# Whole float32 products in place of split ones in decode and retention, and the softmax's chunk factors made by ScalarE alone

## The chip, the cores and the metric

The kernel runs on one core of one Trainium2 chip. The metric is the device time of one execution in microseconds (us); smaller is better. The kernel before took 3410.53 us (median of 3 runs, 3404.25 to 3414.77). Engines are called PE (TensorE, with PEld for its weight loads), DVE (VectorE), ACT (ScalarE), POOL (GpSimd) and SP (SyncE, which issues every DMA here).

## The reference

One layer of a streaming encoder, for a prompt of 2048 tokens and for a batch of 8 decode sequences of 16 new tokens each. All is float32.

```python
h = rms_norm(x, g_norm);  z = h @ w_in
fq, fk, fv, ff, fg, rq, rk, rv, rg, mq, mg, gl = split(z)
# A) forgetting attention: 8 heads x 64, decode has 2048 cached keys
s = fq @ fk.T * 64**-0.5 + c_q - c_k            # c = cumsum(log sigmoid(ff + b_f)), causal
fox_o = softmax(s) @ fv
# B) retention: 4 heads, key width 128, value width 256, in chunks
inter = (q @ s) * dec_q
scores = (q @ k.T) * dmask;  intra = scores @ v
s_new = exp(log_g * L) * s + (k * dec_k).T @ v
# M) attention into 256 memory tokens, 4 heads x 128
mem_o = softmax(mq @ mk.T * 128**-0.5) @ mv
merged = sum_i gate_i * ((branch_i * silu(gate path)) @ w_p_i)
y = x + merged @ w_out
```

The outputs are y, the new keys and values, the log forget gates and the new retention states, for prompt and decode.

## The kernel before

The program has three parts in time. The first makes the input projection for all 17 token tiles (16 of the prompt, one with the 128 decode tokens). The last merges the branches and multiplies by the output weights for the last four of five blocks of tokens. Neither is touched by the change. Between them lies the middle part, where two lanes are woven together: the left lane runs `forget`, `mem_prompt`, `decode_mem`, `decode_fox` and then the first output block; the right lane runs `retention` (16 prompt chunks, then the decode chunk in `sample`) and then `fox`, the prompt's forgetting attention. `weave` advances the lane that is behind by its given total; the builder then orders the instructions of every engine by its own estimate of their times, so that instructions of the lanes lie between one another in each engine's queue, and each engine takes its queue strictly in order. All DMAs go through SP's queue.

TensorE takes float32 data in two ways here. A tile of type F32R is multiplied in one instruction, at reduced precision. To keep precision, an operand is split: h is the value rounded to F32R (a cast by ACT, or by POOL for the decode's values), l = value - h (a subtraction on DVE or POOL), and `mm3` (lines 226 to 228) or `mm3r` (lines 232 to 234) add three products, h by h, h by l and l by h. `split` (line 202 the cast, line 205 the subtraction) is a helper, so these lines stand for many tiles, and the tile's name tells them apart. A tile of type F32 is multiplied as a whole; in the program that is one matmul, and in the profile it is two MATMUL records. Before the change only a few products are whole: the retention's scores (line 1062) and some small sums (lines 1428, 1433, 1451, 1564, 1699).

What the change touches:

- `ret_parts`, lines 1035 to 1056: the transposed q and k of a chunk (`qt`, `kt`), and the split q, k and v (`qh`, `ql` lines 1046 and 1047, `knh`, `knl` lines 1050 and 1051, `vh`, `vl` lines 1054 and 1055). `ret_scores`: the scores in PSUM (`rm`), masked into `sm`, split into `smh`, `sml` (lines 1067 and 1068). `retention.unit`: outputs in PSUM `ry` (line 1138, six products per head), state update in `rm` (three products per head) and `st` (line 1152), which is split again into `sth`, `stl` for the next chunk. `sample` does the same for the 8 decode states, two heads at a time.
- `softmax_scale`, lines 1248 to 1263: where a row's keys come in several chunks of 512, each chunk has its own maximum; DVE takes the difference to the row's maximum (line 1258), ACT the exponential (line 1259), DVE goes on.
- `decode_fox`, lines 1405 onward: for each sequence b, four chunks of 512 cached keys: 16 transposes (line 1500) in groups of four, a split of each group (`dkh`, `dkl`), three products each into `ys`, a softmax, transposes of the probabilities (line 1531) and their split `dpr`, and the product with the values, split by POOL (`dvh` line 1542, `dvl` line 1543), in four matmuls of 256 columns per 128 keys (line 1548).
- `decode_mem`: the same with 256 memory tokens (`mkh`, `mkl`, `mvh`, `mvl`, `mpr`).

## Time and profile before

| | |
|---|---|
| median of 3 runs | 3410.53 us (3404.25 to 3414.77) |
| the profiled execution, its own time | 3406.5 us |
| its span, first to last instruction | 3404.7 us |
| granted TensorE clock, mean of full speed | 0.974 |
| first part (projection), us from the span's start | 0 to 1686 |
| middle part, retention and memory attention | 1686 to 2052 |
| middle part, prompt and decode forgetting attention, first output block | 2052 to 2860 |
| last part (output blocks) | 2860 to 3404.7 |

The borders of the middle part are read from the first and last start of the tiles named above: the first retention transpose starts at 1683.5, the last of `decode_mem` at 2044.2, the last fox product at 2846.5, the second output block's products at 2883.7. The profile gives the busy time of an engine as the union of its instructions' times; matmuls overlap one another, and how much work PE has is rather told by the distance between the starts of matmuls that follow one another without a wait. A wait is put down to the instruction that ended it. The rows themselves stand further down.

### The profile page before, as it was taken

What the parts mean: (1) busy time and instruction counts of PE and PEld (TensorE: products, weight loads), DVE (VectorE), ACT (ScalarE), POOL (GpSimd) and SP (SyncE); (2) the same over time, 40 slices, a digit from 0 to 9 for tenths busy, and PEclk for the clock granted to TensorE, in tenths of its full rate; (3) what the DMA queues carried; (4) which work ended last, traced back from release to release, by engine and by line L of the source; (5) the groups of instructions that cost most, each with busy time, mean ns of one, the idle gap of its engine ahead of it and who ended that gap; (6) DMA issues with size and microseconds to landing.
All of it is one profiled execution on the core that took longest, in us unless ns stands there. A gap on an engine that the chain in (4) does not pass through costs nothing. (4 is left out here: it accounts for less than half of the span.)

```text
span 3404.7 us, 60285 instructions
## 1 busy us (share of the span) xinstructions
PE 3195.5 (94%) x22299; PEld 2997.7 (88%) x22299; DVE 2271.3 (67%) x3732; ACT 1743.5 (51%) x3404; POOL 1217.7 (36%) x1122
## 2 busy tenths in 40 slices
PE   6999999999999999999878888999999988999999
PEld 5998999999999999999868766888887888888899
DVE  7677676665565666565588877887777886545444
ACT  4453444555344555445468755767776764223222
POOL 4436443110220010220176443777776764100000
PEclk8999999999999999999999987999999999999999
DMA  4776566567557667667567765455654457676665
GB/s 166 230 246 201 180 209 198 190 211 253 168 167 215 203 212 244 205 192 220 192 198 230 243 195 162 153 157 162 179 179 148 129 151 224 184 223 204 191 188 166
DMA packets 628219, 660.94 MB, mean 194 GB/s; under 512 B 46060, under 2 KB 549252, under 8 KB 627860
## 3 DMA queue, kind: packets, MB, share of 16 engines
q1 hardware_dynamic: 627924, 657.08, 62.5%
q8 instruction: 176, 2.88, 0.3%
q14 instruction: 119, 0.97, 0.1%
HBM read 477.52 MB, written 179.41 MB: 193 GB/s over the span
## 5 line engine op out<-in xcount | busy, mean ns | idle before, releaser
L400 DVE TENSOR_TENSOR wl<-wr,wh 128x1024 fp32r<-128x1024 f32 (+1 forms) x386 | 568.4, 1476 | 286.9 <-ACT wh L399 282.1
L399 ACT CAST wh<-wr 128x1024 fp32r<-128x1024 f32 (+1 forms) x386 | 404.6, 1050 | 309.9 <-PE b L451 128.0
L449 PE MATMUL a<-wh,ho 128*128 128x256 f32 (+1 forms) x1432 | 408.4, 286 | 18.1 <-ACT gz L707 11.3
L450 PE MATMUL a<-wl,ho 128*128 128x256 f32 (+1 forms) x1432 | 406.3, 284 | 5.8 <-DVE wl L400 5.8
L451 PE MATMUL a<-wh,ho 128*128 128x256 f32 (+1 forms) x1432 | 407.0, 284 | 1.0 <-DVE ho L276 1.0
L428 POOL TENSOR_TENSOR wr<-wr 128x1024 f32<-128x1024 f32 (+1 forms) x72 | 202.1, 2806 | 270.0 <-DMA wr<-in_w_in 235.0
L451 PE MATMUL b<-wh,ho 128*128 128x256 f32 (+1 forms) x1032 | 290.5, 282 | 5.4 <-DVE ho L276 5.4
L449 PE MATMUL b<-wh,ho 128*128 128x256 f32 (+1 forms) x1032 | 291.3, 283 | 4.0 <-ACT wh L399 2.3
L221 ACT CAST wh<-wraw 128x1024 fp32r<-128x1024 f32 x120 | 123.3, 1049 | 334.9 <-DMA wraw<-in_w_p 131.4
L449 PEld LDWEIGHTS a<-wh,ho 128*128 128x128 f32 x1432 | 273.4, 191 | 22.1 <-ACT gz L707 13.7
L450 PE MATMUL b<-wl,ho 128*128 128x256 f32 (+1 forms) x1032 | 290.4, 282 | 0.5 <-DVE wl L400 0.5
L450 PEld LDWEIGHTS a<-wl,ho 128*128 128x128 f32 x1432 | 273.7, 191 | 6.3 <-DVE wl L400 6.3
L451 PEld LDWEIGHTS a<-wh,ho 128*128 128x128 f32 x1432 | 273.7, 191 | 1.5 <-DVE ho L276 1.5
L449 PE MATMUL a<-ho,wh 128*128 128x384 f32 (+1 forms) x768 | 252.6, 329 | 1.6 <-ACT gz L707 1.6
L450 PE MATMUL a<-ho,wh 128*128 128x384 f32 (+1 forms) x768 | 252.9, 329 | 0.0
L451 PE MATMUL a<-ho,wl 128*128 128x384 f32 (+1 forms) x768 | 252.1, 329 | 0.0
L460 ACT COPY kp<-a 128x256 f32<-128x256 f32 (+3 forms) x384 | 153.3, 404 | 183.5 <-PE a L451 182.0
L1334 ACT ACTIVATE pt<-sc,f_mx 128x512 f32<-128x512 f32 (+2 forms) x320 | 201.5, 631 | 73.2 <-DVE f_mx L1333 48.4
L1338 POOL TENSOR_SCALAR pt<-pt,f_f,f_nm 128x512 f32<-128x512 f32 (+3 forms) x288 | 208.6, 740 | 82.2 <-DVE f_nm L1262 28.9
L1333 DVE TENSOR_REDUCE f_mx<-sc 128x1 f32<-128x512 f32 (+2 forms) x320 | 192.6, 604 | 39.4 <-PE sc L1327 21.7
L205 DVE TENSOR_TENSOR pl<-tp,ph 128x512 fp32r<-128x512 f32 (+2 forms) x352 | 193.5, 562 | 34.6 <-ACT ph L202 33.0
L1745 POOL TENSOR_TENSOR gm<-gm,gm 128x512 f32<-128x512 f32 (+2 forms) x40 | 45.6, 1139 | 447.4 <-DVE gm L1743 447.3
(437 smaller groups left out, 9901.0 us busy)
## 6 DMA issues: line engine op xcount, KB each, us to landing
wr<-in_w_in SPq DMA_DIRECT2D x170, 512.0 KB
wraw<-in_w_p SPq DMA_DIRECT2D x80, 512.0 KB
dkt<-in_cache_fox_k SPq DMA_DIRECT2D x64, 512.0 KB
dvt<-in_cache_fox_v SPq DMA_DIRECT2D x64, 512.0 KB
wr<-sum_gl SPq DMA_DIRECT2D x48, 512.0 KB
wraw<-in_w_out SPq DMA_DIRECT2D x40, 512.0 KB
gtd<-gz SPq DMA_DIRECT2D x96, 192.0 KB
gt<-gtd SPq DMA_DIRECT2D x24, 768.0 KB
```

Source lines behind the costliest of these rows:

```text
L205: V.tensor_tensor(l, src, f32(h), ALU.subtract)
L221: S.copy(whv[:, i * hc:(i + 1) * hc], rv)
L399: S.copy(h, t)
L400: eng.tensor_tensor(l, t, f32(h), ALU.subtract)
L428: G.tensor_tensor(out, x, y, op)
L449: T.matmul(out, lh(c), rh(c), start=first and c == 0, stop=False, skip_group_check=True)
L450: T.matmul(out, lh(c), rl(c), start=False, stop=False, skip_group_check=True)
L451: T.matmul(out, ll(c), rh(c), start=False, stop=last and c == 3, skip_group_check=True)
L460: S.copy(t[nm], t["a"])
L1333: V.tensor_reduce(nmx[:, j, ci:ci + 1], sc[:, :w], AX.X, ALU.max, negate=True)
L1334: S.activation(pt[:, :w], sc[:, :w], AF.Exp, bias=nmx[:, j, ci:ci + 1], accum_out=l[:, j, ci:ci + 1])
L1338: G.tensor_scalar(pt, pt, fb, 0.5 if r is None else r[:, j:j + 1], ALU.mult, ALU.mult)
```

## The change

- Decode and retention multiply float32 tiles as whole products. The splits of q, k, v, scores, states, cached keys, cached values and probabilities go there, with the three or six products each; one whole product stands in their place (two MATMUL records each).
- The cached keys of both decode attentions are laid out transposed in the input arrays, on the host, so that the transposes of decode keys go. The DMA of a key tile has the same bytes, in contiguous runs of 2 KB (512 keys) instead of 4 KB, and 1 KB instead of 2 KB for the memory keys.
- The decode queries and new keys that arrive split (`dq`, `dk`, `qms`) are summed once on DVE.
- In `sample`, the masked keys (`kz`) and the placed queries (`qz`) are made by POOL, and the state update takes its decay factor on DVE as it adds.
- In `retention.unit` the state update is now issued ahead of the outputs, and there is one more step (`yield`) before a chunk is stored.
- `softmax_scale`: ACT makes the factor directly, exp(-nmx + nm), with the row's maximum as bias, one instruction per query block; DVE's difference goes.
- Some tiles have more buffers (`rk`, `rv` 4, `dkt` 4, `dvt` 4).

The core of the diff:

```diff
@@ -1032,41 +1032,25 @@
         dma(g, rgd[t * P:(t + 1) * P])
         return g
 
-    def ret_parts(rw, q, k, v):
+    def ret_turn(rw, q, k):
+
+        qt = rw.tile([P, 512], F32, name="qt", bufs=3)
...
-        S.copy(qh, qt)
-        G.tensor_tensor(ql, qt, f32(qh), ALU.subtract)
...
-        S.copy(vh, v)
-        G.tensor_tensor(vl, v, f32(vh), ALU.subtract)
...
-                for n, (dst, l, r) in enumerate(prods):
-                    T.matmul(dst, l, r, start=n == 0, stop=n == len(prods) - 1)
...
-                    mm3(up[:, (h % 2) * 256:(h % 2 + 1) * 256], knh[:, c], knl[:, c], vh[:, vc], vl[:, vc], True, True)
+                for i in range(2):
+                    h = 2 * h2 + i
+                    T.matmul(up[:, i * 256:(i + 1) * 256], k[:, h * P:(h + 1) * P], v[:, h * 256:(h + 1) * 256], start=True, stop=True)
...
-                split(snh, snl, sn)
...
+            for h2 in range(2):
+                op = pry()
+                for i in range(2):
+                    h = 2 * h2 + i
+                    T.matmul(op[:, i * 256:(i + 1) * 256], sm[:, h * P:(h + 1) * P], v[:, h * 256:(h + 1) * 256],
+                             start=i == 0, stop=t == 0 and i == 1)
+                if t:
+                    for i in range(2):
+                        h = 2 * h2 + i
+                        T.matmul(op[:, i * 256:(i + 1) * 256], qt[:, h * P:(h + 1) * P], so[:, h], start=False, stop=i == 1)
...
-                        mm3r(op[:, oc], zb[0][:, i], zb[1][:, i], s0h[:, i], s0l[:, i], False, b == NB - 1 and i == 1)
...
+                        T.matmul(op[:, oc], zb[:, i], s0[:, i], start=False, stop=b == NB - 1 and i == 1)
+                        T.matmul(up[:, oc], zk[:, i * P:(i + 1) * P], v[:, h * 256:(h + 1) * 256], start=True, stop=True)
+                    for i in range(2):
+                        h = 2 * h2 + i
+                        V.scalar_tensor_tensor(sn[:, i], s0[:, i], kc[:, K_GP + 4 + h:K_GP + 5 + h], up[:, i * 256:(i + 1) * 256], ALU.mult, ALU.add)
@@ -1255,8 +1219,8 @@
             return None
         nm = sp.tile([P, 2], F32, name=name + "nm")[:, :nq]
         V.tensor_reduce(nm, nmx, AX.X, ALU.min)
-        V.tensor_tensor(f, nm.unsqueeze(2).broadcast_to([P, nq, ncx]), nmx, ALU.subtract)
-        S.activation(f, f, AF.Exp)
+        for q in range(nq):
+            S.activation(f[:, q], nmx[:, q], AF.Exp, scale=-1.0, bias=nm[:, q:q + 1])
         V.scalar_tensor_tensor(l, l, 2.0, f, ALU.mult, ALU.mult)
-                    for g4 in range(4):
-                        p = pdt()
-                        for j in range(4):
-                            T.transpose(p[:, j * P:(j + 1) * P], kts[j][:, g4 * P:(g4 + 1) * P], ident)
-                        kh = dw.tile([P, 512], F32R, name="dkh", bufs=3)
-                        kl = dw.tile([P, 512], F32R, name="dkl", bufs=3)
-                        split(kh, kl, p)
-                        mm3r(sc, qb[0][:, g4], qb[1][:, g4], kh, kl, g4 == 0, False)
+                    for g2 in range(2):
+                        kt = dw.tile([P, 2, 512], F32, name="dkt", bufs=4)
+                        dma(kt, kv[:, 2 * g2:2 * g2 + 2, ci * 512:(ci + 1) * 512])
+                        for g in range(2):
+                            T.matmul(sc, qb[:, 2 * g2 + g], kt[:, g], start=g2 == 0 and g == 0, stop=False)
...
-                prv = pr.rearrange("p j a r c -> p (j a) r c")[:rows, :2 * n]
-                split(prv[:, :, 0], prv[:, :, 1], p[:rows, :n * P].rearrange("p (a c) -> p a c", c=64))
+                S.copy(pr[:rows, :n], p[:rows, :n * P].rearrange("p (j c) -> p j c", c=P))
...
-                            for i in range(2):
-                                G.tensor_scalar(vh[:, i], vt[:, i], 1.0, 1.0, ALU.mult, ALU.mult)
-                                G.tensor_tensor(vl[:, i], vt[:, i], f32(vh)[:, i], ALU.subtract)
-                        for part in (vh, vl):
-                            for a2 in range(2):
-                                c = slice(a2 * 256, (a2 + 1) * 256)
-                                lt = pr[:, j, a2].rearrange("p r c -> p (r c)")
-                                T.matmul(ov[:, c], lt, part[:, j % 2, c], start=ci == 0 and j == 0 and a2 == 0 and part is vh, stop=False)
+                        T.matmul(ov, pr[:, j], vt[:, j % 2], start=ci == 0 and j == 0, stop=False)
                 else:
...
-        "cache_fox_k": i["cache_fox_k"].reshape(NB, PAST, 512), "cache_fox_v": i["cache_fox_v"].reshape(NB, PAST, 512),
+        "cache_fox_k": i["cache_fox_k"].reshape(NB, P, 16, 4, P).transpose(0, 3, 4, 2, 1).reshape(NB, 4, P, PAST), "cache_fox_v": i["cache_fox_v"].reshape(NB, PAST, 512),
```

The order in which the instructions stand in an engine's queue shows what moves, at three places. First TensorE's queue in the decode's forgetting attention, at a chunk of 512 cached keys among the prompt's scores (`sc`) and values (`ov`); `tp` are transposes, `ys` the decode scores, `dkh` and `dkl` the split keys, `dkt` the whole ones, `qb` the placed queries. Before:

```order
L1500 MATMUL tp<-kc,dkt 128x128 x4
L1380 MATMUL ov<-ph,vv 128x256 x2
L1380 MATMUL ov<-pl,vv 128x256 x2
L234 MATMUL ys<-dkl,qb_23418 128x512
L1360 MATMUL tp<-kc,pt 128x128 x4
L232 MATMUL ys<-dkh,qb_23418 128x512
L233 MATMUL ys<-dkh,qb_23419 128x512
L234 MATMUL ys<-dkl,qb_23418 128x512
L1360 MATMUL tp<-kc,pt 128x128 x4
L232 MATMUL ys<-dkh,qb_23418 128x512
L233 MATMUL ys<-dkh,qb_23419 128x512
L234 MATMUL ys<-dkl,qb_23418 128x512
```

And now:

```order
L1344 MATMUL ov<-pl,vv 128x256
L1344 MATMUL ov<-pl,vv 128x128
L1293 LDWEIGHTS identb
L1293 MATMUL sc<-maskb,identb 128x128
L1460 MATMUL ys<-dkt,qb_22193 128x512 x4
L1461 MATMUL ys<-crow,selr 128x512
L1290 MATMUL sc<-ka,qa 128x512
L1291 MATMUL sc<-kb,qb 128x512
L1344 MATMUL ov<-ph,vv 128x256 x2
```

A group of four transposes and three products, which waited for a cast and a subtraction between them, becomes one product; a chunk's four products now stand together and need only the key tiles and the queries.

Second, TensorE's queue at a retention chunk, among the products of the prompt's memory attention (`m_pt`, `mvN`); `rm` and `ry` are PSUM tiles of the scores or state update and of the outputs. Before, from the second half of a state product to the last output product of one pair of heads:

```order
L227 MATMUL rm<-vl,knh 128x256
L228 MATMUL rm<-vh,knl 128x256
L1138 MATMUL ry<-vh,smh 128x256
L1138 MATMUL ry<-vl,smh 128x256
L1138 MATMUL ry<-vh,smh 128x256
L1138 MATMUL ry<-vl,smh 128x256
L1138 MATMUL ry<-sth,qh 128x256
L1138 MATMUL ry<-sth,ql 128x256
L1138 MATMUL ry<-sth,qh 128x256
L1138 MATMUL ry<-sth,ql 128x256
L1138 MATMUL ry<-vh,sml 128x256 x2
L1138 MATMUL ry<-stl,qh 128x256 x2
```

Now, one pair of heads:

```order
L1050 MATMUL rm<-qt,kt 128x128 x4
L1114 MATMUL rm<-rv,rk 128x256 x2
L1129 MATMUL ry<-rv,sm 128x256 x2
L1134 MATMUL ry<-st,qt 128x256 x2
L232 MATMUL tp<-m_ph,mvN_18526 128x256
L233 MATMUL tp<-m_ph,mvN_18527 128x256
```

Per pair of heads two state products, two of scores by values and two of queries by state stand where eighteen stood, and the state's comes ahead of the outputs. They read `rk`, `rv`, `sm`, `qt` and `st` as these are loaded or computed.

Third, DVE's queue at a softmax of the prompt's forgetting attention; `f_mx` are the chunk maxima, `f_nm` the row's, `f_f` the factors. Before:

```order
L1333 TENSOR_REDUCE f_mx<-sc 128x1
L205 TENSOR_TENSOR dkl<-tp,dkh 128x512
L1257 TENSOR_REDUCE f_nm<-f_mx 128x2
L1258 TENSOR_TENSOR f_f<-f_nm,f_mx 128x2x3
L1260 SCALAR_TENSOR_TENSOR f_l<-f_l,f_f 128x2x3
L1261 TENSOR_REDUCE f_nm<-f_l 128x2
L1262 RECIPROCAL f_nm<-f_nm 128x2
L205 TENSOR_TENSOR dkl<-tp,dkh 128x512
```

Now:

```order
L1297 TENSOR_REDUCE f_mx<-sc 128x1
L1221 TENSOR_REDUCE f_nm<-f_mx 128x2
L1297 TENSOR_REDUCE f_mx<-sc 128x1
L1224 SCALAR_TENSOR_TENSOR f_l<-f_l,f_f 128x2x3
L1297 TENSOR_REDUCE f_mx<-sc 128x1
L1225 TENSOR_REDUCE f_nm<-f_l 128x2
L1351 TENSOR_TENSOR f_ot<-ov,f_ot 64x256
L1226 RECIPROCAL f_nm<-f_nm 128x2
```

The difference to the maximum (`f_f<-f_nm,f_mx`) and the decode's subtractions (`dkl`) are gone from the queue; between the row's maximum and the use of the factors (`f_l<-f_l,f_f`) stands other work, while ACT makes the factors.

## Rows read from the trace of the kernel before

**Rows 1.** The page's second part: the span in 40 equal slices of 85 us, a digit for the busy tenths of a slice; PEclk is the granted TensorE clock in tenths. The middle part is slices 20 to 33.

```profile
PE   6999999999999999999878888999999988999999
...
DVE  7677676665565666565588877887777886545444
ACT  4453444555344555445468755767776764223222
...
PEclk8999999999999999999999987999999999999999
```

**Rows 2.** Busy time by stretch of time, in the order of the table above: the stretch and its length in us, then for each engine busy us (instructions), the granted clock, the DMA engines' busy share and GB/s.

```profile
0.00:1686.00 1686.00, 1617.90 (x11837) 1602.76 (x11837) 1075.12 (x1316) 810.54 (x1314) 401.57 (x176) 0.99 0.65 204
1686.00:2052.00 366.00, 290.13 (x2056) 262.08 (x2056) 290.72 (x713) 244.12 (x534) 209.13 (x197) 0.90 0.72 221
2052.00:2860.00 808.00, 757.23 (x5286) 656.64 (x5286) 631.57 (x1348) 541.02 (x1395) 560.64 (x715) 0.97 0.53 158
2860.00:3404.70 544.70, 530.27 (x3120) 476.19 (x3120) 273.93 (x357) 147.78 (x163) 46.32 (x35) 0.99 0.65 198
```

**Rows 3.** Groups of TensorE's instructions in the middle part (1686 to 2860 us), shapes kept apart: line, engine, operation, out<-in, shape, xcount | busy us, mean ns of one | idle us of the engine just before them, and what ended it.

```profile
L1326 PE MATMUL sc<-ka,qa 128*128 128x512 f32 x224 | 103.3, 461 | 8.2 <-ACT pt L1334 7.8
...
L1500 PE MATMUL tp<-kc,dkt 128*128 128x128 f32 x512 | 79.3, 279 | 0.5 <-PE sc L1327 0.5
L234 PE MATMUL ys<-dkl,qb 128*128 128x512 f32 x128 | 58.1, 454 | 7.3 <-DVE dkl L205 4.3 <-DVE f_nm L1257 3.0
L232 PE MATMUL ys<-dkh,qb 128*128 128x512 f32 x128 | 57.8, 452 | 4.6 <-ACT dkh L202 4.6
L1548 PE MATMUL ym<-dvh,dpr 128*128 128x256 f32 x256 | 52.4, 286 | 2.1 <-DVE dpr L205 2.1
...
L226 PE MATMUL rm<-vh,knh 128*128 128x256 f32 x64 | 21.3, 337 | 10.3 <-ACT vh L1054 6.9 <-DVE sm L1064 3.4
...
L1062 PE MATMUL rm<-qt,kt 128*128 128x128 f32 x136 | 19.6, 291 | 1.7 <-ACT kt L1045 1.7
L227 PE MATMUL rm<-vl,knh 128*128 128x256 f32 x64 | 19.6, 306 | 3.9 <-POOL vl L1055 3.9
```

**Rows 4.** TensorE's instructions in order of time, from three places: a run of 16-column matmuls in the decode's forgetting attention, part of a retention chunk, and a run of 512-column matmuls in the last part. Columns: start us, us from the first start to the last end of the row, engine, line, operation, xcount. Rows left out in between continue the same runs.

```profile
2131.34 0.26 PE L227 MATMUL ys<-dk,qb 128*128 128x16 f32 x1
...
2132.46 0.26 PE L228 MATMUL ys<-dk,qb 128*128 128x16 f32 x1
...
1800.06 1.06 PE L1062 MATMUL rm<-qt,kt 128*128 128x128 f32 x8
...
1801.66 0.28 PE L1138 MATMUL ry<-vh,smh 128*128 128x256 f32 x1
...
1802.50 0.28 PE L1138 MATMUL ry<-sth,ql 128*128 128x256 f32 x1
...
3102.06 0.40 PE L226 MATMUL tp<-ih,wh 128*128 128x512 f32 x1
...
3105.82 0.39 PE L227 MATMUL mr<-il,wh 128*128 128x512 f32 x1
```

**Rows 5.** Groups of DVE's instructions in the middle part, as in rows 3.

```profile
L205 DVE TENSOR_TENSOR dkl<-tp,dkh 128x512 fp32r<-128x512 f32 x128 | 85.6, 684 | 44.1 <-ACT dkh L202 43.6
...
L205 DVE TENSOR_TENSOR stl<-st,sth 128x1024 fp32r<-128x1024 f32 x15 | 23.5, 1566 | 0.6 <-ACT sth L202 0.6
...
L205 DVE TENSOR_TENSOR dpr<-tp,dpr 128x512 fp32r<-128x512 f32 x32 | 21.9, 683 | 3.3 <-ACT dpr L202 3.2
...
L1258 DVE TENSOR_TENSOR f_f<-f_nm,f_mx 128x4 f32<-128x4 f32 x16 | 13.0, 813 | 0.9
L205 DVE TENSOR_TENSOR stl<-st,sth 128x512 fp32r<-128x512 f32 x16 | 12.2, 761 | 4.6 <-ACT sth L202 4.4 <-PE tp L1612 0.2
...
L1258 DVE TENSOR_TENSOR f_f<-f_nm,f_mx 128x6 f32<-128x6 f32 x16 | 9.6, 600 | 0.5
```

**Rows 6.** The same for ACT.

```profile
L202 ACT CAST dkh<-tp 128x512 fp32r<-128x512 f32 x128 | 73.0, 588 | 63.2 <-PE tp L1500 61.0 <-PE ov L1380 0.7
...
L1054 ACT CAST vh<-rv 128x1024 fp32r<-128x1024 f32 x17 | 18.0, 1059 | 9.2 <-DMA rv<-rvd 8.3 <-PE ry L1138 0.9
...
L202 ACT CAST sth<-st 128x1024 fp32r<-128x1024 f32 x15 | 16.0, 1065 | 7.4 <-DVE st L1152 7.4
...
L1259 ACT ACTIVATE f_f<-f_f 128x6 f32<-128x6 f32 x16 | 3.4, 214 | 19.9 <-DVE f_f L1258 19.9
...
L1259 ACT ACTIVATE f_f<-f_f 128x4 f32<-128x4 f32 x16 | 3.4, 210 | 11.7 <-DVE f_f L1258 11.5
```

**Rows 7.** The same for POOL.

```profile
L1543 POOL TENSOR_TENSOR dvl<-dvt,dvh 128x512 fp32r<-128x512 f32 x128 | 161.8, 1285 | 0.5
L1542 POOL TENSOR_SCALAR dvh<-dvt 128x512 fp32r<-128x512 f32 x128 | 77.2, 622 | 51.3 <-PE ym L1548 22.1 <-issue 17.0 <-DMA dvt<-in_cache_fox_v 8.9
...
L1055 POOL TENSOR_TENSOR vl<-rv,vh 128x1024 fp32r<-128x1024 f32 x17 | 44.8, 2635 | 25.7 <-ACT vh L1054 25.4
L1606 POOL TENSOR_SCALAR m_pt<-m_pt,m_l 128x256 f32<-128x256 f32 x64 | 35.9, 575 | 20.1 <-DVE rs_y L197 7.6 <-DVE m_l L1604 6.2 <-DVE gsa L1087 2.8
L1047 POOL TENSOR_TENSOR ql<-qt,qh 128x512 fp32r<-128x512 f32 x17 | 29.5, 1733 | 8.2 <-ACT qh L1046 5.0 <-issue 3.0 <-POOL vl L1055 0.2
```

More of the change, by code (lines that the diff above doesn't have):

```diff
@@ L1174, in unit @@
             yield
+            yield
             ret_store(rw, y, t)
@@ L1195, in sample @@
                     h = 2 * h2 + i
-                    c = slice(h * P, (h + 1) * P)
-                    vc = slice(h * 256, (h + 1) * 256)
-                    mm3(op[:, i * 256:(i + 1) * 256], smh[:, c], sml[:, c], vh[:, vc], vl[:, vc], i == 0, False)
+                    T.matmul(op[:, i * 256:(i + 1) * 256], sm[:, h * P:(h + 1) * P], v[:, h * 256:(h + 1) * 256], start=i == 0, stop=False)
                 if h2:
-                    for z in zs:
-                        for b in (NB - 2, NB - 1):
-                            G.memset(f32(z)[:, b % 2, :, b * TS:(b + 1) * TS], 0.0)
+                    for b in (NB - 2, NB - 1):
+                        G.memset(zq[:, b % 2, :, b * TS:(b + 1) * TS], 0.0)
@@ L1411, in decode_fox @@
             dma(f32(t), f32(d)[:, sc0].rearrange("(g p) t -> p g t", p=P))
+        qw, kw = [dp.tile([P, 4, P], F32, name=f"d{n}w") for n in "qk"]
+        for w, (h, l) in ((qw, qs), (kw, ks)):
+            V.tensor_tensor(w, f32(h), f32(l), ALU.add)
         fg = dp.tile([P, 4, P], F32, name="dfg")
@@ L1453, in decode_fox @@
         V.tensor_copy(cq, cqp[:, :NB])
[L1455 to L1469 removed]
+        qblk = [dp.tile([P, 4, 160], F32, name=f"qb{i}") for i in range(2)]
+        for z in qblk:
+            V.memset(z, 0.0)
+        def unit(b):
+            z = qblk[b % 2]
+            for hf in range(2):
+                rr = slice(64 * hf, 64 * hf + 64)
+                G.tensor_copy(z[rr, :, hf * TS:(hf + 1) * TS], qw[rr, :, b * TS:(b + 1) * TS])
+            qb = z.rearrange("p g c -> p (g c)")[:, :512].rearrange("p (g c) -> p g c", g=4)
             cs = dw.tile([P, 16, 8], F32, name="cs")
@@ L1551, in unit @@
                     dma(f32(vn), f32(vhl)[SEQ + b * TS:SEQ + (b + 1) * TS])
-                    for a2 in range(2):
-                        c = slice(a2 * 256, (a2 + 1) * 256)
-                        lt = pr[:16, 0, a2].rearrange("p r c -> p (r c)")
-                        T.matmul(ov[:, c], lt, vn[:, 4 * a2:4 * a2 + 4, 0:64], start=False, stop=False)
-                        T.matmul(ov[:, c], lt, vn[:, 4 * a2:4 * a2 + 4, 64:128], start=False, stop=a2 == 1)
+                    vw = dw.tile([16, 8, 64], F32, name="dvw", bufs=1)
+                    V.tensor_tensor(vw, f32(vn)[:, :, 0:64], f32(vn)[:, :, 64:128], ALU.add)
+                    T.matmul(ov, pr[:16, 0], vw.rearrange("p h d -> p (h d)"), start=False, stop=True)
                     os = dw.tile([P, 512], F32, name="dos", bufs=1)
@@ L1634, in decode_mem @@
             dma(f32(t), f32(d)[:, sl0].rearrange("(h p) t -> p h t", p=P))
-        qblk = [[dp.tile([P, 4, 80], F32R, name=f"mq{i}{k}") for k in range(2)] for i in range(2)]
-        for zp in qblk:
-            for z in zp:
-                G.memset(f32(z), 0.0)
+        qw = dp.tile([P, 4, P], F32, name="mqw")
+        V.tensor_tensor(qw, f32(qms[0]), f32(qms[1]), ALU.add)
+        qblk = [dp.tile([P, 4, 80], F32, name=f"mq{i}") for i in range(2)]
+        for z in qblk:
+            G.memset(z, 0.0)
         yield
@@ L1670, in unit @@
             for h in range(4):
-                kh, kl = parts[h // 2]
-                c = slice((h % 2) * 256, (h % 2 + 1) * 256)
-                mm3r(sc[:64, :256], qb[0][:, h], qb[1][:, h], kh[:, c], kl[:, c], h == 0, h == 3)
+                T.matmul(sc[:64, :256], qb[:, h], kt[:, h], start=h == 0, stop=h == 3)
             mx = sp.tile([64, 1], F32, name="dm_mx")
@@ L1684, in unit @@
                 T.transpose(p[:, m * 64:(m + 1) * 64], pt[:, m * P:(m + 1) * P], ident[:64, :64])
-            pr = dw.tile([P, 2, 2, 64], F32R, name="mpr")
-            split(pr[:, :, 0], pr[:, :, 1], p[:, :128].rearrange("p (m c) -> p m c", m=2))
+            pr = dw.tile([P, 2, 64], F32, name="mpr")
+            S.copy(pr, p[:, :128].rearrange("p (m c) -> p m c", m=2))
             yield
@@ L1698, in unit @@
             for h in range(4):
-                T.matmul(p[:, h * 64:(h + 1) * 64], os[:, h * P:(h + 1) * P], sumid, start=True, stop=True)
+                T.transpose(p[:, h * 64:(h + 1) * 64], os[:, h * P:(h + 1) * P], ident[:64, :64])
             for h in range(4):
```

168 lines of the change are left out of this document (43 added, 125 removed).

## The prediction

> **What bounds the kernel now.** I read the busy digits over the span first, then the busy time by stretch, then TensorE's groups in the middle part, and last its starts in order of time. The digits of TensorE stand at 9 in the first and last part and fall to 8 and 7 only in the middle, where DVE and ACT rise to 7 and 8 [rows 1]. The busy time by stretch says the same: in the first part TensorE is busy 1617.9 of 1686 us, in the last 530.3 of 544.7, in the two stretches of the middle 290.1 of 366 and 757.2 of 808 [rows 2]. The change touches the middle alone, so the 2230.7 us of the other two parts stay.
>
> The middle is 1174 us. Busy there, adding the two stretches: TensorE 1047, DVE 922, ACT 785, POOL 770 us [rows 2]. Busy time flatters TensorE, since its matmuls overlap. What it has to do I count by the distance of starts in runs without waits: 0.235 us for 512 columns (16 steps from 3102.06 to 3105.82), 0.120 for 256 (7 steps from 1801.66 to 1802.50), and 0.112 for 16 columns (10 steps from 2131.34 to 2132.46), which is thus the floor of one instruction [rows 4]. The middle has 2056 + 5286 = 7342 matmul records [rows 2], of which 384 (decode keys) and 2 times 224 (the prompt's scores, whose second product has the same width) have 512 columns [rows 3]: 832 at 0.235 is 195 us, the other 6510 at some 0.117 are 762. So TensorE has about 957 us of work in 1174 us, and some 217 us go by in waits, short and long. DVE is at 79% of that time, ACT at 67%: no engine is full, each waits its turn in another's queue. The waits that show as idle are a little of many kinds: cast and subtraction of the decode keys 4.6 and 4.3, casts and subtractions of the values in retention 6.9 and 3.9, the softmax before the scores 7.8 [rows 3].
>
> **The change, part by part.** TensorE loses, from the counts of the loops: 384 key products (90.2 us at 0.235), 512 key transposes (57.3 at 0.112), 512 value products of 256 columns (61.4 at 0.120), 564 products in the prompt's retention (67.7) and 204 in the decode's (24.5), in the decode's memory attention 64 transposes, 96 products of 256 and 32 of 512 columns (26.2), and small ones (new keys and values, folding sums) 28.9. Together 356 us.
>
> It gains whole products: 280 of 512 columns (128 keys, 128 + 8 values, 16 memory values) and 288 of 256 columns (188 and 68 in retention, 32 in memory scores), two records each, and 18 us of small ones at the floor. What a record of a whole product costs at these widths the trace does not show; its only run has 128 columns: eight records from 1800.06 on take 1.06 us to the last end, one of them some 0.28, so seven steps of 0.112 us [rows 4]. That is the floor, which also 16 columns pay, so it does not tell what the columns cost. From below: a record streams like a split one, 0.235 and 0.120; then 280 x 0.470 + 288 x 0.240 + 18 = 219 us, 137 less than what goes. From above: the 0.112 is all columns and grows with them, 0.448 for 512 and 0.224 for 256; then 280 x 0.896 + 288 x 0.448 + 18 = 398 us, 42 more than goes. I take the upper end, since the one row of a whole product lies on it: 128 columns cannot take less than what was seen, and nothing in the trace shows a whole product going at the split one's rate per column.
>
> The Trainium skill has a rule that speaks against this change: "FP8 and Floating Point Precision", TensorE Precision Notes, says that true float32 takes four passes through the array, where the split form makes three products. By that rule and the rows' 0.235 a whole product of 512 columns would take 0.94 us, and TensorE would gain 63 us instead of 42. No row of this case shows a product wide enough to confirm it; the row of 128 columns does not contradict it.
>
> The other engines lose work in the same middle part. DVE: the subtractions for keys 85.6, states 23.5 and 12.2, probabilities 21.9, and the factor differences 13.0 and 9.6 [rows 5], 166 us of 922 by the rows shown; the smaller ones that go, and the small sums that come, I let cancel. ACT: the casts of keys 73.0, of values 18.0 and of states 16.0 [rows 6], 107 of 785; it gains 48 exponentials at 0.21 [rows 6], 10 us. POOL: the split of the decode values 161.8 and 77.2, of the retention's values 44.8 and queries 29.5 [rows 7], 313 of 770; the masked keys it takes over cost 16 times 0.58, by its 256-column operation of the same kind [rows 7], 9 us.
>
> What the additions wait for: the decode retention's masked keys and placed queries come from POOL now, and the state products stand behind them in TensorE's queue. In full on the path that would be the 9 us and as much for the copies; at nothing if POOL is early. POOL is busy 209 of 366 us there [rows 2] and loses the splits, so I count nothing, with 18 us as the other end. The two exponentials per softmax wait for the row's maximum and stand in ACT's queue; now ACT stands idle 19.9 and 11.5 us for DVE's difference [rows 6], a step that goes. The key tiles come in runs half as long. The DMA engines are busy 0.53 of the long stretch and 0.72 of the retention's [rows 2]; 37.7 MB of keys (72 tiles of 128 x 1024 values) among the 808 us x 158 GB/s = 128 MB would, at twice the time per byte, bring 0.53 to 0.69. So I count nothing for it. The retention's own floor by DMA is 0.72 x 366 = 264 us.
>
> The state's chain in retention gets shorter by a cast and a subtraction, 1.07 and 1.57 us per chunk [rows 5, 6], and the decode keys' by four transposes, cast and subtraction per group. What is late next is the softmax of the prompt's attention (scores, maximum, exponential, factors, POOL's scaling, transposes, split), which the change leaves, but for its factors.
>
> The sum: TensorE 957 + 42 = 999 us of work, DVE 756, ACT 688, POOL 466. The 217 us of waits shrink. At the least, a quarter goes, which is more than the waits named on removed work; at the most three quarters, which would bring the middle near the first and last part, where TensorE hardly waits. I take half, 108: the queues that TensorE waits on carry a sixth (DVE), an eighth (ACT) and two fifths (POOL) less, and the longest chains lose links. The middle is then 999 + 108 = 1107 us, 67 less than 1174. The profiled execution, 3406.5 us, becomes 3339.5; the median of the runs shown lies 4.0 above it, so the forecast is 3343.5, say 3343. With a quarter gone it is 55 later (3398), with three quarters 54 earlier (3289).
>
> **The rivals.** First, the whole product is cheap: each record streams like a split one, and TensorE's work falls to 820 us. For it: the rows cannot tell it from the dear one. Against: only that the one row of a whole product lies on the upper end. The other engines would bound sooner, DVE's 756 us would again be near three quarters of the time, and I leave the waits at 217: 1037, 137 less, 3273.
>
> Second, the waits stay and the work comes on top. The place is TensorE's queue in the long stretch, where it is busy 757 of 808 us [rows 2]: whole products of 0.9 us stand in order ahead of the prompt's scores and values, and what TensorE waits for is the length of the softmax's chain and not the load of DVE or ACT. Then 957 + 42 + 217 = 1216, 42 more: 3452. It decides where less than a fifth of the waits goes (42 of 217). For it: of the idle that shows, only 19.7 us (4.6, 4.3, 6.9, 3.9) are put down to work that goes [rows 3]. Against: the subtraction that ended a wait on the prompt's side stood in the same queue behind the decode's.
>
> Third, a wash: the waits shrink by about the 42 us that TensorE gains, the work moves from DVE, ACT and POOL to TensorE and the time stays, 3400 to 3420.
>
> **How the numbers follow.** The forecast, dear products with half of the waits gone, has 0.68, with its own range 3289 to 3398. Cheap products 0.08, the wash 0.09, more work with the same waits 0.15. About 0.3% (10 us) is what a measurement can tell from no change. All of the first two is faster, 0.76, and a little of the wash, 0.01; the rest of the wash, 0.08, is the same; slower is 0.15. The range of 8 in 10 takes in the wash and reaches down to the cheap products' edge: 3275 to 3415.
>
> **What would show it.** Whole products: the distance of starts of two records of 512 columns in the decode's key products; near 0.45 or above says dear, near 0.235 cheap. Waits: the middle's length, with TensorE's digits rising from 8 to 9 in slices 24 to 33 while DVE's fall to 6 or 7. The long stretch should lose some 20 to 40 us and the retention's about as many; DVE's total should fall by 166 us or more, POOL's by 300. First and last part should be as long as now. The forecast is wrong if records of 512 columns take much over 0.47 us, if the first part or last part changes, or if TensorE's waits in the long stretch keep their size with the softmax's exponentials and scalings as their releasers.

## The result, and the profile after

The changed kernel took 3370.08 us (median, 3369.22 to 3384.07), the kernel before 3409.36 us beside it: a ratio of 0.9894, 95% interval 0.9864 to 0.9924, so some 39 us faster. The forecast was 3343 us with a range of 3275 to 3415: the time lies inside, the sign is right, and of the 67 us forecast somewhat over half came. The profiled execution is the slowest of the four (span 3382.3 us); a second profile, of the same kernel run again below, has a span of 3372.1 us.

The page's digits after, of the same five rows as in [rows 1]:

```profile
PE   6998999999999999999979979999999999999999
...
DVE  7676676756555666565567736555555676554444
ACT  4453444545444455445446535655565674222222
POOL 4446443110220010220001213333333353100100
PEclk8999999999999999999989988999999999999999
```

TensorE stands at 9 almost everywhere in the middle, DVE fell to 5 to 7 and POOL to 3 in the long stretch. Busy time by stretch, columns as in [rows 2], the stretches cut near the same events (1690, 2019, 2836):

```profile
0.00:1690.00 1690.00, 1619.93 (x11837) 1604.49 (x11837) 1075.00 (x1315) 809.22 (x1312) 401.93 (x177) 0.99 0.65 204
1690.00:2019.00 329.00, 287.44 (x1663) 238.14 (x1664) 202.02 (x579) 165.39 (x412) 54.77 (x133) 0.92 0.81 249
2019.00:2836.00 817.00, 783.20 (x4400) 572.38 (x4399) 501.45 (x1147) 494.85 (x1319) 323.57 (x447) 0.97 0.53 157
2836.00:3382.00 546.00, 527.40 (x3075) 472.57 (x3074) 268.93 (x352) 143.68 (x159) 43.76 (x34) 0.99 0.64 195
```

Against [rows 2] the retention's stretch went from 366 to 329 us, and the long one did not get shorter at all, though in it DVE lost 130 us, ACT 46 and POOL 237. TensorE's busy share rose there (757 of 808 to 783 of 817), which looks better and is not: the records of whole products overlap more.

The cuts of these windows are rounded, so I measure the stretches by two events of TensorE: the retention's from its first transpose to the last fold of the decode's memory attention, the long one from there to the last product of the prompt's probabilities and values. And since busy time flatters, I take TensorE's starts apart: the distance from a record to the next is work up to 0.01 us above its median over all records of the same line and shape, and waiting beyond it. (Some numbers on record below, 705 and 650 us of work, are the same count over the wider windows.) All of it is worked out from the starts in the one trace of each kernel, in us; the kernels were timed on several chips, each beside the kernel before (3406.0 to 3410.2 us), so times are best compared by their ratios:

| kernel | time, median | ratio to before | retention's stretch | long stretch | its work + waits | behind it |
|---|---|---|---|---|---|---|
| before | 3409.4 | 1 | 360.7 | 802.3 | 693 + 109 | 558 |
| after | 3370.1 | 0.9894 | 326.6 | 801.8 | 692 + 110 | 565 |
| e1_again | 3375.2 | 0.9904 | 327.5 | 802.3 | 692 + 110 | 560 |
| e2_v_split | 3349.7 | 0.9837 | 325.2 | 773.7 | 640 + 134 | 565 |
| e3_k_half | 3315.7 | 0.9730 | 325.4 | 742.8 | 638 + 105 | 563 |
| e4_dve_back | 3399.0 | 0.9974 | 322.8 | 829.4 | 695 + 135 | 564 |
| e5_ret_only | 3371.3 | 0.9886 | 325.6 | 807.7 | 692 + 115 | 557 |
| e6_fox_only | 3410.2 | 1.0009 | 358.0 | 801.0 | 691 + 110 | 560 |
| e7_softmax_old | 3380.7 | 0.9917 | 325.5 | 801.3 | 692 + 109 | 565 |
| e8_sc3 | 3420.0 | 1.0032 | 330.7 | 829.8 | 698 + 132 | 573 |
| e9_grain | 3377.8 | 0.9907 | 324.8 | 805.6 | 693 + 112 | 565 |
| e10_v_split_act | 3343.5 | 0.9803 | 324.6 | 778.7 | 652 + 126 | 555 |
| e11_ret_load | 3372.4 | 0.9889 | 324.2 | 807.4 | 692 + 116 | 563 |
| e12_v_split_mk | 3334.9 | 0.9786 | 315.2 | 770.5 | 642 + 129 | 564 |

In the retention's stretch the count is 241 + 120 before and 252 + 75 after. So the whole gain is there: 11 us more work, 45 us less waiting. In the long stretch neither number moved. The part behind it, which only one of the runs below touches, is 555 to 565 us long in the others, so a few us of a profile's span come from there. By this count a record at the lower level of TensorE's clock counts as waiting too: in the 2 us pieces of the retention's stretch with a granted clock under 0.75, excesses of up to 1.1 times the median sum to 13 us before and 12 after, so the clock is not what changed there.

What a whole product costs is now in the trace. TensorE's starts in order of time, from the decode's keys (two products of 512 columns are four records) and from a chunk of retention (256 columns); columns as in [rows 4]:

```profile
2118.86 3.60 PE L1460 MATMUL ys<-dkt,qb 128*128 128x512 f32 x8
2122.39 0.49 PE L1461 MATMUL ys<-crow,selr 16*128 16x512 f32 x1
...
1760.70 1.02 PE L1114 MATMUL rm<-rv,rk 128*128 128x256 f32 x4
1761.57 1.03 PE L1129 MATMUL ry<-rv,sm 128*128 128x256 f32 x4
1762.43 1.03 PE L1134 MATMUL ry<-st,qt 128*128 128x256 f32 x4
```

Eight records of 512 columns take 3.53 us to the next line's start (with some 0.1 us for the step to it), four of 256 take 0.86 to 0.87. Over all pairs of neighbours in the trace the median distance is 0.429 us for 512 columns and 0.216 for 256: 0.858 and 0.432 for a whole product, in two records each.

Which engines wait for each other in the long stretch, before (2052 to 2860 us) and after (2019 to 2836 us): engine, tile and line, what it waited for, us in total, times, longest. Before:

```profile
ACT pt L1334 <- DVE f_mx L1333: 45.7, 61, 5.5
DVE pl L205 <- ACT ph L202: 31.8, 54, 2.3
ACT ph L202 <- PE tp L1360: 31.1, 52, 1.6
POOL pt L1338 <- DVE f_nm L1262: 27.9, 12, 5.9
```

After, the same four:

```profile
DVE pl L205 <- ACT ph L202: 102.8, 105, 4.0
ACT ph L202 <- PE tp L1324: 98.5, 76, 3.5
POOL pt L1302 <- DVE f_nm L1226: 91.1, 22, 14.7
ACT pt L1298 <- DVE f_mx L1297: 65.4, 85, 6.3
```

These are the links of one chain, the prompt's attention: scores, maximum, exponential, factors, scaling, transposes, cast, subtraction, product. Before, the engines of that chain had the decode's splits to do between two links; after, they stand idle for each other. TensorE's own largest wait in these windows is for the same chain, before:

```profile
PE sc L1326 <- ACT pt L1334: 12.5, 14, 5.1
```

And after:

```profile
PE sc L1290 <- ACT pt L1298: 14.1, 28, 1.3
```

The count by starts says more, when each wait is put down to the product that follows it. Ahead of the transposes and products of the decode's cached keys the waits fell from 21 to 7 us; ahead of the prompt's scores, transposes and value products they rose from 66 to 83. The waits of the keys' chain went, and as much came back ahead of the prompt's products. For 60 of the 109 us before and 41 of the 110 after the profile shows idle time with a releaser; the rest is longer distances under overlapping records, and what TensorE waited for there is not shown.

### The profile page after: what moved, and what is told of

Its sections match the earlier page's. It is cut to its first block, busy times and chain, and to the rows that moved or that the text cites. A ratio compares the mean times of both kernels' runs of the same rounds, so it can differ in the third digit from the quotient of the medians.

```text
span 3382.3 us, 56779 instructions
## 1 busy us (share of the span) xinstructions
PE 3218.0 (95%) x20971; PEld 2887.6 (85%) x20971; DVE 2047.4 (61%) x3390; ACT 1613.1 (48%) x3201; POOL 824.0 (24%) x789
## 4 chain that ended last, share of the span: by engine, by line
PE 70%; DMA 13%; DVE 7%; issue 4%; ACT 3%; POOL 2%; SPq 1%; DVEq 0%; ACTq 0%; POOLq 0%
PE a L449 7%; PE a L451 7%; PE a L450 7%; PE b L449 5%; PE b L451 5%; PE b L450 5%; PE ov L1344 3%; PE tp L1324 3%; PE ys L1460 3%; PE ym L1494 3%; DMA out_y_p<-x 3%; DMA x<-in_x_prompt 2%; PE sc L1290 2%; DVE wl L400 2%; PE sc L1291 1%
## 5 line engine op out<-in xcount | busy, mean ns | idle before, releaser
L202 ACT CAST ph<-tp 128x512 fp32r<-128x512 f32 (+2 forms) x352 | 167.5, 490 | 119.4 <-PE tp L1324 99.9
```

The source lines that it names most:

```text
L202: S.copy(h, src)
```

## The experiments

**The changed kernel again**, unchanged, as the base for the others.

> The changed kernel once more, for its time, its spread and a second profile. All theories: 3370 us, within 6, about 0.9885 of the kernel before; two records of a whole 512-column product start 0.43 us apart; retention stretch about 330 us, the stretch of the two forgetting attentions about 800 to 817 against 808 before.

Measured: 3375.2 us, ratio 0.9904 (0.9885 to 0.9922). The two middle stretches agree with the first profile to 1 us, so a difference of 5 us and more in one of them is taken seriously below.

**Values split again, keys whole.** The decode's probabilities and values are split as in the kernel before, all else is as after.

```diff
-                        T.matmul(ov, pr[:, j], vt[:, j % 2], start=ci == 0 and j == 0, stop=False)
+                            for i in range(2):
+                                G.tensor_scalar(vh[:, i], vt[:, i], 1.0, 1.0, ALU.mult, ALU.mult)
+                                G.tensor_tensor(vl[:, i], vt[:, i], f32(vh)[:, i], ALU.subtract)
+                        for part in (vh, vl):
+                            for a2 in range(2):
...
+                                T.matmul(ov[:, c], lt, part[:, j % 2, c], start=ci == 0 and j == 0 and a2 == 0 and part is vh, stop=False)
```

> The changed kernel with the decode values and probabilities split as before (four matmuls of 256 columns per 128 keys instead of one whole product), keys still whole. Theory A (TensorE's own work sets the long stretch, and the load of DVE, ACT and POOL does not): 128 x (0.858 - 0.480) = 48 us less, about 3322. Theory B (waits follow the load of DVE and POOL, as the prediction had it): the 24 us on DVE and 239 us on POOL come back and with them much of the waits, 3350 to 3370. Theory C (the prompt's softmax chain, step after step, sets the long stretch whatever TensorE does beside it): 3370.

Measured: 3349.7 us, 0.9837 (0.9814 to 0.986), faster than both kernels. TensorE's work in the long stretch falls by 52 us, near 128 x (0.858 - 4 x 0.120) = 48, and its waits rise by 24, with 231 us more of POOL's work and 47 more of DVE's than in e1.

**Half of the key products left out.** Of each pair of head groups only the first is multiplied, so the decode's scores lack half of their sum.

```diff
-                        for g in range(2):
-                            T.matmul(sc, qb[:, 2 * g2 + g], kt[:, g], start=g2 == 0 and g == 0, stop=False)
+                        T.matmul(sc, qb[:, 2 * g2], kt[:, 0], start=g2 == 0, stop=False)
```

> The changed kernel without every second product of the cached keys (two of the four groups of heads are left out of the decode scores; loads as before): 64 x 0.858 = 55 us less work on TensorE and nothing else changed. Theory A: 3315. Theory B: 3315 or a little below. Theory C: 3365 to 3370.

Measured: 3315.7 us, 0.973 (0.9707 to 0.9752). 64 products of 0.858 us are 55 us; the stretch lost 59, and the waits hardly moved (110 to 105). With the other engines' load as it is after, TensorE's work counts one for one: theory A's point, and theory C falls.

**DVE's key work put back, unused.**

```diff
+                            V.tensor_tensor(dw.tile([P, 512], F32, name="dld", bufs=1), kt[:, g], kt[:, g], ALU.subtract)
```

> The changed kernel with DVE given back the time of the removed key subtractions: one 128x512 subtraction into an unused tile beside each key product, 128 in all, some 88 us of DVE in the long stretch; nothing reads them. Theory A: 3370, within 10. Theory B: the waits grow again, 3390 to 3410. Theory C: 3370.

Measured: 3399.0 us, 0.9974 (0.9957 to 0.9991): 24 us slower than e1, all of it in the long stretch's waits (110 to 135). So what was put into DVE's queue does cost, as B has it. That it costs by its load is not shown: the added subtractions also stand in DVE's queue until the key tile's DMA has landed, and DVE sits idle 58.9 us for that.

**Each half of the change alone.** In the first, the kernel before with `retention` and `decode_mem` of after; in the second, with `decode_fox` of after. The softmax's factors stay as before in both.

```diff
+            qt, kt = ret_turn(rw, q, k)
...
+                    T.matmul(up[:, i * 256:(i + 1) * 256], k[:, h * P:(h + 1) * P], v[:, h * 256:(h + 1) * 256], start=True, stop=True)
```

```diff
+                        for g in range(2):
+                            T.matmul(sc, qb[:, 2 * g2 + g], kt[:, g], start=g2 == 0 and g == 0, stop=False)
...
+                        T.matmul(ov, pr[:, j], vt[:, j % 2], start=ci == 0 and j == 0, stop=False)
```

> The kernel before with whole products in retention and in the decode's memory attention alone; the decode's forgetting attention and the softmax's factors are as before. Theory D (all of the gain is in the retention stretch, 34 us, and the long stretch gives nothing): 3372, ratio 0.990, retention stretch 327 us, long stretch 802. Theory E (the long stretch gains from the softmax or the decode and loses as much to something else that came with it): the long stretch moves, by 15 us or more either way.

> The kernel before with whole products in the decode's forgetting attention alone; retention, memory attention and softmax as before. Theory D: the same as before, 3406 within 8, long stretch 802. Theory E: 3406 plus or minus 15 or more; if the softmax's factors are what helped in the changed kernel, this one is slower than before, 3420.

Measured: 3371.3 us, 0.9886 (0.9865 to 0.9907), and 3410.2 us, 1.0009 (0.9996 to 1.0021). Retention and memory carry the whole gain, as theory D has it; whole products in the decode's forgetting attention, 128 key tiles and 128 value tiles of them, are worth nothing together. With e2 this splits: whole keys take 53 us of work off (693 to 640) and the waits grow by 25; whole values put 52 back and the waits fall by 24. The change thus has two edits of opposite sign in this stretch.

**The softmax's factors as before**, the rest as after.

```diff
-        for q in range(nq):
-            S.activation(f[:, q], nmx[:, q], AF.Exp, scale=-1.0, bias=nm[:, q:q + 1])
+        V.tensor_tensor(f, nm.unsqueeze(2).broadcast_to([P, nq, ncx]), nmx, ALU.subtract)
+        S.activation(f, f, AF.Exp)
```

> The changed kernel with the softmax's factors made as before (difference on DVE, exponential on ACT). Theory D: 3375, the same as the changed kernel. Theory E with the softmax as what helped: 3385 to 3395. If ACT's extra instruction hurts: 3365 or less.

Measured: 3380.7 us, 0.9917 (0.9902 to 0.9933), 5 us above e1, with intervals that overlap and a long stretch of the same length. A few us at most.

**Three PSUM banks for the prompt's scores**, taken from its transposes (three to two).

```diff
-                psum_more(st, "right", sc=2, ov=1)
+                psum_more(st, "right", sc=3, ov=1)
...
-        psum_pools(st3, tp=3)
+        psum_pools(st3, tp=2)
```

> The changed kernel with three PSUM banks for the prompt's scores instead of two, and two for transposes instead of three. Theory F (the waits of the long stretch are mostly the prompt's scores waiting for a bank until the exponential has read it, 23 us before sc and what follows from it): 20 to 30 us less, 3345 to 3355. Theory G (they come from the order and from the whole chain maximum, exponential, factors, scaling, transposes, split): within 10 of 3375, or slower, since transposes lose a bank.

Measured: 3420.0 us, 1.0032 (1.0018 to 1.0045), 45 us slower than e1. Of the profile's extra 49 us, 27 are in the long stretch and 14 behind it, where output products use the transposes' banks too. Theory F falls in this form: a bank for scores bought with one of the transposes costs more than the score's wait. In the long stretch ACT's exponentials now wait 85.0 us for the transposes. A bank added without taking one was not tried.

**Whole products in halves.**

```diff
-                        T.matmul(ov, pr[:, j], vt[:, j % 2], start=ci == 0 and j == 0, stop=False)
+                        for c in (slice(0, 256), slice(256, 512)):
+                            T.matmul(ov[:, c], pr[:, j], vt[:, j % 2, c], start=ci == 0 and j == 0 and c.start == 0, stop=False)
```

> The changed kernel with each of the decode's whole key and value products made in two halves of 256 columns (0.216 us a record by the profile of after) where it was one of 512 (0.429 us a record): the same columns and the same sums, but the blocks that stand between the prompt's products in TensorE's queue are half as long. Theory G: the long stretch keeps its 108 us of waits because the whole products hold the prompt's score products and transposes up by some 0.86 us at a time, on a chain that is late already; then halves let them in sooner and the time falls by 10 to 20 us against the changed kernel (3375), to 3355 to 3365. Theory H: the order in TensorE's queue is fixed by the program and nothing slips in between; the length of one product is nothing to the chain, and the time stays within 5 us, or rises by up to 10 for the 256 more instructions.

Measured: 3377.8 us, 0.9907 (0.9884 to 0.993), the long stretch 3 us longer, as H has it. For the keys this is a test of G: with the edit other products come between the halves, and the median run of key products from its first start to the next other record falls from 3.5 us (8 records) to 1.1. Shorter key blocks bring nothing. For the values it is not: 27 of their 39 runs still hold 16 halves, four whole products, and a median run takes 3.3 us where it took 3.4. Whether the length of the value blocks holds the prompt's scores up stays open.

**Split values with ACT's cast.** As e2, with the rounding moved from POOL to ACT.

```diff
+                            S.copy(vh, vt)
                             for i in range(2):
-                                G.tensor_scalar(vh[:, i], vt[:, i], 1.0, 1.0, ALU.mult, ALU.mult)
                                 G.tensor_tensor(vl[:, i], vt[:, i], f32(vh)[:, i], ALU.subtract)
```

> The kernel with whole key products and split decode values, in which ScalarE makes the value's rounded half by one copy of 128x1024 for each pair of tiles and GpSimd keeps only the subtractions. In that kernel's run (3349.7) the long stretch had 650 us of TensorE work and 130 us of waits, against 705 and 110 with whole values. Theory I: the 22 us of waits came back with GpSimd's 230 us more of work (553 against 322 us in the long stretch), because GpSimd makes the prompt's masked keys behind it; with about half of that work gone from GpSimd some 10 us of the waits go, to 3335 to 3345. Theory J: ScalarE stands on the prompt's chain of exponentials itself, and 64 copies of about 0.9 us there cost more than GpSimd's did: 3355 to 3375.

Measured: 3343.5 us, 0.9803 (0.9783 to 0.9823). The time fits theory I, but its interval overlaps that of e2, and the profile does not bear it out: the long stretch is 779 us against 774, and what is shorter is the part behind it, which the edit does not touch. Undecided.

**The retention's state split, unused.**

```diff
+            if t < 15:
+                split(rw.tile([P, 4, 256], F32R, name="sth"), rw.tile([P, 4, 256], F32R, name="stl"), sn)
```

> The changed kernel with the two halves of the retention's state still made for each of 15 chunks, by ScalarE (about 1.07 us) and VectorE (about 1.57 us) as in the kernel before, and read by nobody: the load of that edit without its place in the chain. The retention's stretch of 327 us was 361 before. Theory K: it got shorter because the state reaches its products without the two steps in between, which stand one behind the other; then the unused halves leave it at 327 to 332 and the time at 3375 to 3380. Theory L: it got shorter because the two engines had less to do there; then the stretch grows by 15 to 40 us (2.64 us for each of 15 chunks is 40), and the time to 3390 to 3415.

Measured: 3372.4 us, 0.9889 (0.9871 to 0.9907), the retention's stretch 324.2 us. The two groups are there, DVE's and ACT's, and cost nothing:

```profile
L205 DVE TENSOR_TENSOR stl<-st,sth 128x1024 fp32r<-128x1024 f32 x15 | 18.3, 1221 | 6.0 <-ACT sth L202 6.0
...
L202 ACT CAST sth<-st 128x1024 fp32r<-128x1024 f32 x15 | 15.8, 1051 | 7.6 <-DVE st L1119 7.6
```

L falls for this edit: DVE's and ACT's load was not what the stretch was long for. Of the two K is left: it is the place of these steps between the state and its products that cost, or else something else that went with them. The splits of values, queries, keys and masked scores were not put back one by one; the state update issued ahead of the outputs, the additional `yield` and the four buffers for `rk` and `rv` were not tried apart either. So which of them gave how much of the 34 us stays open.

**Four buffers for the memory's key tiles.** As e2, with this line:

```diff
-            kt = dw.tile([P, 4, 256], F32, name="mkt")
+            kt = dw.tile([P, 4, 256], F32, name="mkt", bufs=4)
```

> The kernel with whole key products and split decode values, with four buffers for the key tiles of the decode's memory part in place of its two. In the changed kernel's profile TensorE waits 15.4 us there for the DMA of such a tile. Theory M: the load starts late because a buffer comes free late; with two more the wait goes, and the time falls by 10 to 15 us from 3349.7, to 3335 to 3340. Theory N: the load starts late because its queue or the DMA engines are busy with the decode's tiles; then the wait stays or moves to the tiles behind it, and the time stays within 5 us of 3349.7.

Measured: 3334.9 us, 0.9786 (0.9758 to 0.9813), the fastest kernel that leaves nothing out, 2.1% below the kernel before. TensorE's wait at this place, in after:

```profile
PE ys L1598 <- DMA mkt<-in_cache_mem_k: 15.4, 3, 8.7
```

In e2, without the edit:

```profile
PE ys L1611 <- DMA mkt<-in_cache_mem_k: 14.3, 3, 8.8
```

With it:

```profile
PE ys L1611 <- DMA mkt<-in_cache_mem_k: 10.1, 3, 7.4
```

The retention's stretch is 10 us shorter. Theory M, in part: 4.2 us of the wait itself went, some of the rest with it (the eight loads are issued within 24.5 us instead of 38.4), and 10.1 us of the wait are still there. The longest of the three, 7.4 us, is for the first tile, whose load had a free buffer in e2 already.

## Why the forecast was right, and where its steps were off

**Which product is dear.** Right: the upper end was taken, 0.448 and 0.224 us a record from the floor of 128 columns, and 0.429 and 0.216 were measured. The rival of cheap products (0.235) is out. That it held is in part luck: by the forecast's own words the row of 128 columns lies on a floor that 16 columns pay too and does not tell the two apart. The Trainium skill's rule in "FP8 and Floating Point Precision", TensorE Precision Notes, four passes for true float32, agrees in kind: 0.858 us is 3.65 times the split product's 0.235, and the estimate by that rule, 0.94, is 10% too much.

**TensorE's added work, forecast +42.** Mis-sized: +11 in the retention's stretch and -1 in the long one, so +10. Two terms explain it. The gain was 280 x 0.038 + 288 x 0.016 = 15 us too high by the measured records. And the loss was too low: the removed key products were priced at 0.235 each, while by their starts in the trace of before the first and the third of each three took 0.313 and 0.317, which is 128 x 0.16 = 20 us more. 42 - 15 - 20 = 7. Why these two are slower is not shown; the first of the prompt's two score products takes 0.316 as well, before and after, and the forecast's 957 us priced it at 0.235.

**The retention's waits.** Right. "The retention's about as many", 20 to 40 us, was 34. Of the waits on removed work that it named, the 3.9 us on the values' subtraction [rows 3] are gone. The 6.9 us on their cast are not: the cast itself had waited for the load of `rv` [rows 6], and after the change TensorE waits for that load directly, 7.2 us at the same place. e11 rules out that the load of the state's split was the cause. One new wait came that the forecast did not name, 15.4 us for the memory's key tiles: the tiles had two buffers, and the DMA engines are busy 0.81 of that stretch against 0.72 [rows 2]. That is the same DMA time in a shorter stretch, 266 us against 264, and in the long one 433 against 428, so the shorter runs of the key tiles cost the DMA engines nothing that shows, as the forecast took it.

**The long stretch's waits.** This is the step that failed: "I take half, 108", from the relief of the queues. Over both stretches 45 of 229 us went, a fifth, and none in the long one, where 20 to 40 us were to be lost. One of the forecast's own signs of being wrong came true here: the waits of the long stretch kept their size (109 and 110), with the prompt's exponentials as the largest releaser that shows. The time still lies in the range because two misses work against each other: 63 us too many were put down for the waits that go, and 32 us too many for the work that comes. That part is luck. The condition of the second rival (less than a fifth of the waits goes) holds there, though its price did not come due, since TensorE's work did not rise. Two things lay behind it. First, the forecast summed decode keys and values as one change; taken apart, whole keys free TensorE of 512 transposes (57 us at 0.112) while 128 whole products (110 us at 0.858) cost as much as the 384 that they replace, and whole values cost 48 us against a split that POOL paid for, with DVE and ACT for the probabilities. Second, the waits that the removed chain had caused came back ahead of the prompt's products, 14 us fewer against 17 more. That load on DVE and POOL can matter, e2 against e3 shows (640 and 638 us of work with 134 and 105 us of waits), and e4 points the same way; no run had fewer than 105 us of waits in this stretch. Why before, with the most load of all, had no more than 109 us is not settled: its 53 us more of TensorE's work may have filled what would have been waits.

**The digits.** TensorE's went to 9 and DVE's to 5 to 7 in those slices, about as forecast, and yet the stretch stayed. The forecast offered them as a sign that waits went; they are not one, since a record of a whole product shows 0.59 us of busy time and lets the next start after 0.43. DVE's total fell by 224 us (at least 166 forecast), POOL's by 394 (300). The other end for the masked keys, 18 us on POOL, did not show: no wait of TensorE in the decode's retention is put down to `kz` or `qz`.

## What to carry to other kernels

Price each operand of a split product by itself: making it whole pays where the split also costs TensorE something else (the keys' transposes) or seems to lie in a chain that TensorE waits for (retention, where the link was not isolated), and loses where an engine with time to spare made the halves (the values on POOL). Less load on engines that are not full need not shorten anything; ask which chain the waits belong to, and whether a link of it goes. And judge TensorE by the distance of its starts, not by its busy digits.

## What the runs showed of the hardware

The softmax's difference on DVE, six numbers a row, was priced at its mean of 0.60 to 0.81 us [rows 5]. Its median is 0.17 us; a few took very long. One of them in the kernel before, in DVE's order of time:

```profile
2578.94 0.14 DVE L1257 TENSOR_REDUCE f_nm<-f_mx 128x2 f32<-128x6 f32 x1
2579.19 5.32 DVE L1258 TENSOR_TENSOR f_f<-f_nm,f_mx 128x6 f32<-128x6 f32 x1
2584.78 0.17 DVE L1260 SCALAR_TENSOR_TENSOR f_l<-f_l,f_f 128x6 f32<-128x6 f32 x1 [0.27 <-ACT f_f L1259]
```

And POOL's, at the same time:

```profile
2578.42 2.37 POOL L1542 TENSOR_SCALAR dvh<-dvt 128x512 fp32r<-128x512 f32 x4
2580.77 3.72 POOL L1543 TENSOR_TENSOR dvl<-dvt,dvh 128x512 fp32r<-128x512 f32 x3
```

The small operation ends when POOL's run of seven ends. The Trainium skill, "SBUF — State Buffer", Who interferes with whom, states that a DVE instruction with two SBUF inputs contends with a GpSimd instruction that reads SBUF; the trace agrees, and the hold lasts longer than one instruction of POOL's, which stood back to back. Of the 48 differences 16 took over 0.4 us before, and 31 us in all; in e6, with whole values, 2 and 9 us. The stall goes with POOL's split, not with the difference: where the values are split again and the difference is gone, the next operation of that kind has it. The factors' product `f_l` in after:

```profile
L1224 DVE SCALAR_TENSOR_TENSOR f_l<-f_l,f_f x48: 152/165/1492, 2012.1 to 2795.6; 128x4 f32<-128x4 f32 x16, 128x6 f32<-128x6 f32 x16, 128x8 f32<-128x8 f32 x16
```

And in e2 (min, median and max in ns):

```profile
L1224 DVE SCALAR_TENSOR_TENSOR f_l<-f_l,f_f x48: 145/184/3424, 2003.0 to 2758.4; 128x4 f32<-128x4 f32 x16, 128x6 f32<-128x6 f32 x16, 128x8 f32<-128x8 f32 x16
```

Its sum is 10.2 us in after, 31.0 in e2, and 18.1 in e10, where POOL keeps only the subtractions. It stands on the prompt's chain: a place where some of e2's 24 us of waits may come from. A form of the value's split that leaves POOL out altogether was not tried. The same shows in the retention: the subtraction `stl` of 128 x 1024 took 1.57 us in the mean before [rows 5], with POOL busy 209 of 366 us, and 1.22 us in e11 above, with POOL busy 54 of 324. Taken one by one in before, the five with POOL busy for at most 0.15 of their time took 1.19 to 1.23 us, the other ten 1.21 to 3.34.
